# The first stage of a two-layer hybrid backbone: loads and stores put in another order on one queue

## The chip, the cores and the metric

The kernel runs on one core of one Trainium2 chip. The metric is device time in microseconds. A core has TensorE (matmul, PE in the profile), VectorE (DVE), ScalarE (ACT), GpSimd (POOL), and SyncE (SP), whose queue issues the DMAs of this kernel. The engines run their own instruction lists in order and meet through semaphores.

## The reference

The reference is a two-layer backbone over 1024 latent tokens and 256 context tokens of width 1024. Cut to what matters here:

```python
sc, scc = silu(c), silu(c_ctx)
# layer 0: convolution branch and gated linear recurrence, side by side
shift, scale, gate = split(sc @ mod_w[0] + mod_b[0], 3)
hx = rmsnorm(x, norm_g[0]) * (1 + scale) + shift
hc = rmsnorm(ctx, norm_g[0]) * (1 + scale_c) + shift_c      # same weights, from scc
z = hx @ ev_w_in                       # va, vg, ga, xb, gb
y_a = silu(layernorm(conv31(va * sigmoid(vg)))) * silu(ga)
y_b = rglru(conv4(xb), h0=from context) * silu(gb)
x = x + gate * (concat(y_a, y_b) @ ev_w_out)
# layer 1: pooling mixer
u, g = split(h @ od_w_in, 2)
d = multiscale_pool(u)                 # 4 groups
y = einsum("bngi,gij->bngj", d, od_w_grp) * od_scale
x = x + gate * ((y * silu(g)) @ od_w_out)
return rmsnorm(x, final_g)
```

Pooling is linear, so the kernel multiplies the `u` half of `od_w_in` with `od_w_grp` ahead of time; this product is called the fold. Two of its four groups are folded in the first stage.

## The kernel before, in words

Matrix products run in a split form: a 32-bit operand becomes a high and a low part (`split`, L102: ScalarE casts the high part, VectorE or GpSimd subtracts to get the low one), and a product is three matmuls: high by high, high by low, low by high.

Almost all of the text is about the first stage, L274 to L435, which ends with the first matmuls of the even layer (L672 on). What it does:

- Fold of groups 0 and 1 (`fold`, L238). A group loads two matrices `graw`, splits them into `gh` and `gl`, and then takes four weights `wu`, each of which is loaded and split by `wload` (L117) and used for two products of 12 matmuls (L260 to L262). A product is copied from PSUM by ScalarE (`fo`, L265) and stored to DRAM (`wfold`). Group 0's low parts come from VectorE, group 1's from GpSimd. `fold` is a generator; `fold_some(n)` runs its next n pieces, and a group has five: the group matrices, and one piece a weight.
- Tokens. `x_load` (L365) loads 128 of the 1024 columns of `x` as a tile `x_k`, and sums squares on ScalarE and VectorE. `rstd_cols` (L197) turns the sums into factors spread over all partitions (`ms_x`): column sums on TensorE, the root on ScalarE (`rc_x`), a diagonal on VectorE (`dg_x`), and one matmul.
- Modulation. `mod_loads` (L318) loads a block of `mod_w` and multiplies it with the SiLU of `c` and `c_ctx` (`modr`); `mod_cols` (L330) copies the result to a row (`modrow`), turns it into columns (`modt`), and writes shift and scale into `m0` and `a0`. There are four blocks of four loads, and each serves two token tiles. `modulate` (L343) writes the split tokens `h0h` and `h0l`.
- Context tokens. `ctx_load`, `ctx_scale` and `ctx_split` (L381 to L394) do the same for the 256 context tokens: `sq_c` is their root, `cx` the tokens, `cth` and `ctl` the split parts.
- The even layer's first weights: `xb`, whose product is made for latent tokens (`xb`) and context tokens (`xbc`), then `vg` and `va`. `uc` is the short convolution of `xb`; it is split into `uh` and `ul` for the gate products `g`.
- Gate dots. The third part of the first layer's modulation, which nothing reads before the output projection, is made by eight VectorE dot products of `modT` tiles with the SiLU of `c`, spread over all partitions (`cL`). Before, the spread is made at the very front by two matmuls (L378), and the dots run in the even layer's first turn (L711 to L718), where their tiles are those of the recurrence (`l`).

The order of the work is set in two ways. A scheduler orders the instructions of each engine by its own estimate of times. On SyncE's queue, loads made by `load` (L109) in the first stage are chained: each is issued after the load that stands before it in the program. The fold's stores are not part of that chain; they are put on the queue by the scheduler. From L444 on, the order on VectorE, ScalarE, GpSimd and TensorE is that of the program (`on`, L440).

Weights go through a pool of two buffers for each kind: raw (`wr`), high (`wh`) and low (`wl`). A load of a raw weight is issued once the raw weight two places ahead has been split.

Of the kernel before, what the change touches and what calls it, by code (L numbers as in the profile page):

```python
# [56 lines left out]
def body(ctx, tc, xT, ctxT, cc, ccol, modT, modW, win, gw, wout, wu, grp, wg, wo1, small, edge, ident, outT):  # L57
# [49 lines left out]
    chain = [None]  # L107

    def load(out, src):  # L109
        with ExitStack() as lctx:  # L110
            if chain[0] is not None:
                lctx.enter_context(tc.issue_after(chain[0].ins))
            d = nc.sync.dma_start(out, src)
            if chain[0] is not None:
                chain[0] = d
# [29 lines left out]
    nc.sync.dma_start(sm, small)  # L145
    eg = base.tile([P, 4 * 16], F32, name="eg")
    nc.sync.dma_start(eg, edge)
# [23 lines left out]
    nc.scalar.activation(sa, lam, AF.Abs)  # L171
    nc.scalar.activation(sa, sa, AF.Exp, scale=-1.0)
    nc.vector.tensor_scalar(out=sb, in0=sa, scalar1=2.0, scalar2=None, op0=add)
    nc.vector.reciprocal(sb, sb)
    nc.vector.tensor_tensor(out=sz, in0=sa, in1=sb, op=mult)
    nc.vector.tensor_tensor(out=sb, in0=sz, in1=sz, op=mult)
    nc.vector.memset(sa, 1.0 / 17.0)
    for n in range(7, -1, -1):
        nc.vector.tensor_tensor(out=sa, in0=sa, in1=sb, op=mult)
        nc.vector.tensor_scalar(out=sa, in0=sa, scalar1=1.0 / (2 * n + 1), scalar2=None, op0=add)  # L180
    nc.vector.tensor_tensor(out=sa, in0=sa, in1=sz, op=mult)
    nc.vector.tensor_scalar(out=sb, in0=lam, scalar1=-1.0, scalar2=0.0, op0=mult, op1=ALU.max)
    nc.vector.scalar_tensor_tensor(out=sa, in0=sa, scalar=2.0, in1=sb, op0=mult, op1=add)
    nc.vector.tensor_scalar(out=chalf, in0=sa, scalar1=4.0, scalar2=None, op0=mult)
    nc.vector.tensor_scalar(out=cneg, in0=sa, scalar1=-8.0, scalar2=None, op0=mult)
# [52 lines left out]
    def fold(g, raw_tile, out_tile, g_tile=None, w_tile=None):  # L238
        g_tile = g_tile or dtile
        gh, gl = [], []  # L240
        for i in range(2):
            raw = raw_tile(f"graw_{g}_{i}")
# [10 lines left out]
        for kp in range(KT // 2):  # L253
            wh, wl = (wload(wu[g, kp], f"wu_{g}_{kp}", nc.vector if g == 0 else nc.gpsimd)
                      if w_tile is None else ws[kp])
            for s in range(2):
                ps = psum(f"fold_{g}_{kp}_{s}")
                for i in range(4):
# [7 lines left out]
                (nc.sync if g < 2 else nc.scalar).dma_start(dst[:, :, s, :].rearrange("m p c -> p m c"),  # L266
                                    o.rearrange("p (m c) -> p m c", c=P))
# [4 lines left out]


# [5 lines left out]
    with ExitStack() as sctx:  # L279
# [117 lines left out]
        for k in range(3):  # L397
            x_load(k)
# [1370 lines left out]
```

## Time and profile before

| | us |
|---|---|
| time, median of 3 runs | 1304.87 |
| the three runs | 1301.92, 1304.87, 1305.92 |
| the profiled execution's own time | 1306.04 |
| its span, first to last instruction | 1304.0 |
| TensorE busy in the span | 1267.2 (97%) |
| VectorE busy | 1132.8 (87%) |
| ScalarE busy | 646.1 (50%) |
| GpSimd busy | 300.2 (23%) |

A row of the timeline gives start and duration in us, the engine and the line, the operation, output and inputs by the program's names, shapes, count, and in brackets the idle time before it and what ended that. In the views by windows the columns are the window, and for each engine its busy time and instructions; then the granted TensorE clock (1.00 is full speed), the busy share of the DMA engines, and GB/s. A row whose engine ends in q (SPq) is an issue on a queue, not the transfer. In the list of DMA issues the last figure of a row is the median time from issue to landing. The mean granted clock of the profiled execution is 0.993.

### The profile page before, as it was taken

The numbers are of one execution on the slowest core, as the hardware profiler recorded it, in microseconds if no ns is written. First come the engines' busy times: TensorE is split into PE (matmuls) and PEld (weight loads), VectorE is DVE, ScalarE is ACT, GpSimd is POOL, SyncE is SP. The second block draws the span as 40 slices with busy tenths as digits, with TensorE's granted clock in tenths as the row PEclk, the third lists the DMA queues.
The fourth block names the chain that finished last, engine by engine and source line by source line (L and its number), as shares of the span: only waits on it lengthen the run. The fifth ranks groups of instructions, "written<-read, shape, count | busy, mean of one in ns | idle before, by whom it ended". The sixth has DMA issues, their size and how long they took to land.

```text
span 1304.0 us, 16066 instructions
## 1 busy us (share of the span) xinstructions
PE 1267.2 (97%) x5780; PEld 1036.4 (79%) x5780; DVE 1132.8 (87%) x1756; ACT 646.1 (50%) x935; POOL 300.2 (23%) x151
## 2 busy tenths in 40 slices
PE   7999999999999999999999999999999999999995
PEld 5687888888888887888887778788888888788784
DVE  6669999999999999978968959999999987977776
ACT  7443666566566633236535346634343434645442
POOL 0212644364535546543210022000000000000002
PEclk9999999999999999999999999999999999999997
DMA  9953111122011233442418566334333334868623
GB/s 360 337 178 112 57 42 64 52 62 69 37 57 57 81 127 124 154 145 89 147 47 287 181 195 178 106 121 154 121 126 101 121 113 137 309 217 281 214 85 129
DMA packets 82865, 181.81 MB, mean 139 GB/s; under 512 B 7777, under 2 KB 27617, under 8 KB 82786
## 3 DMA queue, kind: packets, MB, share of 16 engines
q1 hardware_dynamic: 74338, 176.60, 39.9%
q10 hardware_dynamic: 8448, 4.20, 1.1%
q8 instruction: 45, 0.74, 0.2%
q14 instruction: 34, 0.28, 0.1%
HBM read 136.72 MB, written 44.04 MB: 139 GB/s over the span
## 4 chain that ended last, share of the span: by engine, by line
PE 55%; DVE 29%; DMA 8%; issue 3%; ACT 3%; POOL 1%; SPq 0%; POOLq 0%; ACTq 0%; DVEq 0%
DVE conv L444 7%; PE wob L444 6%; PE vg L444 5%; PE va L444 4%; PE xb L444 4%; DVE l L444 4%; PE g L444 3%; DMA yr_t<-y_t 2%; PE fold L262 2%; PE fold L260 2%; PE fold L261 2%; PE ga L135 2%; PE ga L444 2%; PE ga L134 2%; PE ga L136 2%
## 5 line engine op out<-in xcount | busy, mean ns | idle before, releaser
L444 DVE SCALAR_TENSOR_TENSOR conv<-u,sm,conv 128x505 f32<-128x505 f32 (+6 forms) x224 | 153.5, 745 | 1.0
L1588 POOL TENSOR_TENSOR o<-x,rr 128x256 f32<-128x256 f32 (+1 forms) x9 | 8.0, 925 | 452.6 <-ACT rr L1576 449.6
L444 ACT ACTIVATE l<-g,sm 128x512 f32<-128x512 f32 (+1 forms) x96 | 58.7, 618 | 60.0 <-PE g L444 59.2
L104 POOL TENSOR_TENSOR wl_wu<-wr_wu,wh_wu 128x1024 fp32r<-128x1024 f32 x12 | 28.7, 2390 | 171.5 <-ACT wh_wu L103 128.1
L260 PE MATMUL fold<-gh,wh_wu 128*128 128x512 f32 x128 | 53.2, 416 | 4.9 <-ACT wh_wu L103 4.9
L444 POOL TENSOR_TENSOR l<-l,l 128x1280 f32<-128x1280 f32 x16 | 47.1, 2965 | 25.6 <-ACT l L444 15.1
L444 PE MATMUL wob<-ybl,wh_wob 128*128 128x512 f32 x128 | 50.1, 392 | 2.3 <-POOL ybl L444 2.3
L261 PE MATMUL fold<-gl,wh_wu 128*128 128x512 f32 x128 | 51.7, 404 | 0.0
L262 PE MATMUL fold<-gh,wl_wu 128*128 128x512 f32 x128 | 50.3, 405 | 0.3 <-POOL wl_wu L104 0.3
L444 PE MATMUL gb<-h0h,wl_gb 128*128 128x512 f32 x128 | 49.9, 390 | 0.2 <-POOL wl_gb L444 0.2
L444 PE MATMUL gb<-h0l,wh_gb 128*128 128x512 f32 x128 | 49.8, 389 | 0.0
L444 PE MATMUL wob<-ybh,wh_wob 128*128 128x512 f32 x128 | 49.8, 389 | 0.0
L444 PE MATMUL gb<-h0h,wh_gb 128*128 128x512 f32 x128 | 49.8, 389 | 0.0
L444 PE MATMUL vg<-h0h,wh_vg 128*128 128x512 f32 x128 | 49.8, 389 | 0.0
L444 PE MATMUL vg<-h0l,wh_vg 128*128 128x512 f32 x128 | 49.8, 389 | 0.0
L444 PE MATMUL wob<-ybh,wl_wob 128*128 128x512 f32 x128 | 49.8, 389 | 0.0
L444 PE MATMUL vg<-h0h,wl_vg 128*128 128x512 f32 x128 | 49.8, 389 | 0.0
L444 PE MATMUL va<-h0h,wh_va 128*128 128x512 f32 x128 | 49.8, 389 | 0.0
L444 PE MATMUL va<-h0l,wh_va 128*128 128x512 f32 x128 | 49.8, 389 | 0.0
L444 PE MATMUL va<-h0h,wl_va 128*128 128x512 f32 x128 | 49.8, 389 | 0.0
L444 DVE TENSOR_TENSOR_SCAN l<-l,l 128x256 f32<-128x256 f32 (+1 forms) x32 | 48.7, 1521 | 1.1
L103 ACT CAST wq_g<-wr_g 128x512 fp32r<-128x512 f32 x48 | 28.2, 620 | 40.9 <-DVE wr_g L887 12.9
(593 smaller groups left out, 4291.4 us busy)
## 6 DMA issues: line engine op xcount, KB each, us to landing
wr_wu<-wu SPq DMA_DIRECT2D x16, 512.0 KB, 4.5
modw<-modW SPq DMA_DIRECT2D x16, 512.0 KB, 7.1
x_part<-xp SPq DMA_DIRECT2D x32, 256.0 KB, 2.4
mod<-modT SPq DMA_DIRECT2D x32, 256.0 KB, 3.7
wr_v<-wfold SPq DMA_DIRECT2D x16, 512.0 KB, 3.6
wr_g<-wg SPq DMA_DIRECT2D x16, 512.0 KB, 4.4
wr_wo<-wo SPq DMA_DIRECT2D x16, 512.0 KB, 4.6
yr_t<-y_t SPq DMA_DIRECT2D x16, 512.0 KB, 5.9
```

The source lines that it names most:

```text
L103: return (nc.scalar.copy(hi, src), eng.tensor_tensor(out=lo, in0=src, in1=hi.bitcast(F32), op=sub))
L104: eng.tensor_tensor(out=lo, in0=src, in1=hi.bitcast(F32), op=sub))
L134: nc.tensor.matmul(ps, hi[:, kc], xh[k][:, cols], start=(k == 0), stop=False)
L135: nc.tensor.matmul(ps, hi[:, kc], xl[k][:, cols], start=False, stop=False)
L136: nc.tensor.matmul(ps, lo[:, kc], xh[k][:, cols], start=False, stop=(k == ks - 1))
L260: nc.tensor.matmul(ps, wh[:, kc], gh[i], start=(i == 0), stop=False)
L261: nc.tensor.matmul(ps, wh[:, kc], gl[i], start=False, stop=False)
L262: nc.tensor.matmul(ps, wl[:, kc], gh[i], start=False, stop=(i == 3))
L444: last[eng] = f(*args, **kw)
L1588: nc.gpsimd.tensor_tensor(out=o[:, k - k0], in0=v, in1=rr, op=mult)
```

## The change

It changes the first stage and moves two pieces of work into it or within it:

- The front of the queue becomes: group matrix, first fold weight, second group matrix, second fold weight, two token tiles, third fold weight, and so on. The small tables (`sm`, `eg`, `idx`) go to later places, and with `sm` the decay rates of the recurrence, now a function called in the middle of the stage.
- The fold's stores of groups 0 and 1 are no longer placed by the scheduler. They are collected in a list, and `store_folds(n)` puts the next n on the chained queue: group 0's after later weights, group 1's eight all together at the end of the stage.
- A modulation block's four loads are made in one piece, after the two `modulate` calls of the block before; some of the last block's loads take buffers of another pool.
- `xb` is loaded ahead of group 1's last fold weight; `vg` and `va` are loaded within the chain of the first stage.
- The gate dots move from the even layer's first turn to the end of the first stage, and take token buffers. `cL` is loaded from DRAM as a broadcast instead of being spread by matmuls.
- Ten small matmuls on a tile of ones run at the start. The low part of group 1's first weight goes to VectorE. Two pools get more buffers (6 to 8, and 6 to 7).

Cut to its core (the decay rates are the same instructions, now within `decay_rates()`):

```diff
@@ fold @@
-        gh, gl = [], []
+        gh, gl, early = [], [], None
         for i in range(2):
+            if g == 0 and i == 1:
+                early = wload(wu[g, 0], f"wu_{g}_0", nc.vector)
             raw = raw_tile(f"graw_{g}_{i}")
             load(raw, grp[g, i])
...
-            wh, wl = (wload(wu[g, kp], f"wu_{g}_{kp}", nc.vector if g == 0 else nc.gpsimd)
-                      if w_tile is None else ws[kp])
+            if kp == 0 and early is not None:
+                wh, wl = early
+            elif w_tile is None:
+                wh, wl = wload(wu[g, kp], f"wu_{g}_{kp}", nc.vector if g == 0 or kp == 0 else nc.gpsimd)
+            else:
+                wh, wl = ws[kp]
...
-                (nc.sync if g < 2 else nc.scalar).dma_start(...)
+                if g < 2:
+                    stores.append((dst, o))
+                else:
+                    nc.scalar.dma_start(dst, o)
...
+    def store_folds(n):
+        while n and stores:
+            load(*stores.pop(0))
+            n -= 1
...
+        warm = psum("warm")
+        for i in range(10):
+            nc.tensor.matmul(warm[:, :P], ones, ones, start=True, stop=True)
+
+        def spread_c():
+            load(cL, cc[0].partition_broadcast(P))
+            nc.scalar.activation(cL, cL, AF.Silu)
+
+        def gates():
+            for m in range(2 * KT, 3 * KT):
+                raw = xtile(f"mod0_{m}")
+                load(raw, modT[0, m])
+                nc.vector.scalar_tensor_tensor(out=raw, in0=raw, scalar=1.0, in1=cL, op0=mult, op1=mult,
+                                               accum_out=m0[:, 0, m : m + 1])
...
-        fold_some(2)
-        for k in range(3):
+        fold_some(3)
+        for k in range(2):
             x_load(k)
         fold_some(1)
-        for k in range(3, 7):
+        load(ccv, ccol)
+        nc.scalar.activation(cpad[:, :, 0:2], ccv, AF.Silu)
+        for k in range(2, 5):
             x_load(k)
+        store_folds(2)
         fold_some(1)
-        x_load(7)
-        mod_loads(0, range(3))
+        load(idx, ident)
+        load(sm, small)
+        for k in range(5, 8):
+            x_load(k)
+        store_folds(2)
+        mod_loads(0, range(2))
+        fold_some(1)
+        mod_loads(0, range(2, 4))
         rx = [rstd_cols(acc[h][:, :H], f"x{h}", idx, spool, h) for h in range(2)]
         fold_some(1)
-        mod_loads(0, range(3, 4))
+        store_folds(4)
         mod_cols(0)
...
+        mod_loads(1, range(4))
+        decay_rates()
         fold_some(1)
+        mod_cols(1)
         modulate(2)
         modulate(3)
+        mod_loads(2, range(4))
         fold_some(1)
+        mod_cols(2)
         modulate(4)
         modulate(5)
+        mod_loads(3, range(4))
+        w_xb0 = wload(win[3 * KT], "xb0", nc.vector)
         fold_some(1)
+        mod_cols(3)
         modulate(6)
         modulate(7)
-        w_xb0 = wload(win[3 * KT], "xb0", nc.vector)
         ctx_load(0)
         ctx_load(1)
+        w_vg0 = wload(win[KT], "vg0", nc.vector)
         ctx_scale()
         ctx_split(0)
         ctx_split(1)
-        chain[0] = None
+        raw_va0 = wpool.tile([P, D], F32, tag="wr", name="wr_va0")
+        load(raw_va0, win[0])
+        spread_c()
+        store_folds(8)
+        gates()
+        load(eg, edge)
+        chained[0] = False
```

More of the change, by code (lines that the diff above doesn't have):

```diff
@@ L294, in fold_some @@
                 next(folds, None)
-        cx = [spool.tile([P, D], F32, name=f"cx_{i}") for i in range(2)]
+        cx = []
         xs = []
@@ L677, in body @@
         mm3(xc, w, (ch, cl), slice(0, C))
-        w = wload(win[KT], "vg0", nc.gpsimd)
+        w = w_vg0
         uc = utile("uc0")
```

80 lines of the change are left out of this document (28 added, 52 removed).

## The prediction

> **What bounds the kernel now.** I read the page's busy times and slices first, then TensorE's timeline of the first 125 us, then the other engines' timelines and the queue's at the same places, and last the windows for the clock.
>
> ```profile
> span 1304.0 us, 16066 instructions
> ...
> PE 1267.2 (97%) x5780; PEld 1036.4 (79%) x5780; DVE 1132.8 (87%) x1756; ACT 646.1 (50%) x935; POOL 300.2 (23%) x151
> ...
> PE   7999999999999999999999999999999999999995
> ```
>
> TensorE is the bound, but its busy share says little, since a matmul's record overlaps the next one's. So I go by the distance from one start to the next, and by the points of the first stage at which the changed kernel can be compared with this one.
>
> ```profile
> 10.29 0.80 PE L260 MATMUL fold<-gh,wh_wu 128*128 128x512 f32 x1 [2.90 <-ACT wh_wu L103]
> ...
> 15.15 0.63 PE L260 MATMUL fold<-gh,wh_wu 128*128 128x512 f32 x1
> 15.58 0.63 PE L261 MATMUL fold<-gl,wh_wu 128*128 128x512 f32 x1
> ...
> 17.20 0.39 PE L260 MATMUL fold<-gh,wh_wu 128*128 128x512 f32 x1
> 17.43 0.39 PE L261 MATMUL fold<-gl,wh_wu 128*128 128x512 f32 x1
> ...
> 45.85 1.07 PE L326 MATMUL modr<-modw,cpad 128*32 128x256 f32 x16
> ...
> 51.52 0.95 PE L335 MATMUL modt<-sm,modrow 128*128 128x2 f32 x8
> ...
> 53.30 0.50 PE L260 MATMUL fold<-gh,wh_wu 128*128 128x512 f32 x1 [0.27 <-ACT wh_wu L103]
> ...
> 55.77 0.50 PE L262 MATMUL fold<-gh,wl_wu 128*128 128x512 f32 x1 [0.27 <-POOL wl_wu L104]
> ...
> 72.38 0.48 PE L260 MATMUL fold<-gh,wh_wu 128*128 128x512 f32 x1
> ...
> 89.30 0.28 PE L134 MATMUL xbc<-cth,wh_xb 128*128 128x256 f32 x1
> ...
> 97.40 0.28 PE L135 MATMUL xbc<-ctl,wh_xb 128*128 128x256 f32 x1
> 97.52 0.28 PE L136 MATMUL xbc<-cth,wl_xb 128*128 128x256 f32 x1
> ...
> 103.56 0.39 PE L444 MATMUL va<-h0h,wl_va 128*128 128x512 f32 x1
> ...
> 117.69 0.39 PE L444 MATMUL xb<-h0h,wl_xb 128*128 128x512 f32 x1
> 119.97 0.50 PE L444 MATMUL g<-uh,wh_gw 128*128 128x512 f32 x1 [1.89 <-DVE u L444]
> ```
>
> The reader is to see three things. A 512-column matmul starts 0.227 us after the one before (17.20 to 17.43), but 0.43 us after it at first (15.15 to 15.58): the thirteen steps from 10.29 on lose 2.9 us. From 10.29 on TensorE hardly waits: 0.27 us twice in those rows, and 2.28 - 0.23 = 2.05 us ahead of 119.97. A step of 256 columns is 0.12 us (97.40 to 97.52). And after the first stage TensorE stands at nine tenths or more in every slice but the last, so what the first stage gains or loses by the `g` matmul at 119.97 is taken as the change of the time. That point is my yardstick.
>
> **The front of the queue.** The loads go on one queue in program order.
>
> ```profile
> 0.74 0.40 SPq L145 DMA_DIRECT2D sm<-small  x1
> ...
> 3.85 0.43 SPq L113 DMA_DIRECT2D wr_wu<-wu  x1
> ```
>
> ```profile
> 10.00:20.00 10.00, 9.71 (x31) 7.71 (x32) 8.35 (x15) 8.24 (x15) 0.00 (x0) 1.00 1.03 412
> ```
>
> The first fold weight is issued at 3.85 us, behind five small loads and both group matrices. In the changed kernel it is the second issue, one place of 0.47 us behind 0.74, thus 2.64 us earlier, and one 512 KB transfer less lies ahead of it: 1.27 us at 412 GB/s. The fold starts at 10.29 - 3.9 = 6.4 us, say 6.5. The vector work of the decay rates and the spread of `c` leave the front too; they delay nothing that counts, as ScalarE's cast releases the fold, not they.
>
> **The first group's fold.** Four weights of 24 matmuls, 96 x 0.227 = 21.8 us, with 0.3 us for the first low part: it ends at 28.6 us. Before, token sums and modulation matmuls lay between these; now they come behind them, as the changed order of TensorE's instructions shows.
>
> **The middle, 28.6 to 37.0 us.** Here the changed order is serial. Sums of squares, their root on ScalarE, the diagonal on VectorE, its product, the second half of the first modulation block, `modrow`, and only then the cast of the second group's first weight.
>
> ```profile
> 31.19 1.28 ACT L204 ACT_TABLE_LOAD   x1
> 32.51 0.26 ACT L204 ACTIVATE rc_x<-ms_x,eps_r 128x4 f32<-128x4 f32 x1
> ```
>
> ```profile
> 33.02 0.69 DVE L207 TENSOR_TENSOR dg_x<-idx,rc_x 128x512 f32<-128x512 f32 x1
> ```
>
> ```profile
> 50.05 0.57 ACT L332 COPY modrow<-modr 128x512 f32<-128x512 f32 x1
> ...
> 52.20 1.05 ACT L103 CAST wh_wu<-wr_wu 128x1024 fp32r<-128x1024 f32 x1
> ```
>
> Copy of the last fold 0.6, table 1.3, two roots and two diagonals of about 0.26 + 0.2 + 0.69 each, 2.3; the last diagonal's product 0.9 (an estimate: four 0.23 us passes); two loads' modulation matmuls 1.1; `modrow` 0.6; cast 1.05; some 0.1 us at each of five handovers: 8.4 us, so the second group starts at 37.0. In before the same links are hidden behind the fourth fold weight; that cover is gone. The data are there by then. A load of 512 KB that has little beside it lands 3.5 us after its issue:
>
> ```profile
> wr_xb<-win SPq DMA_DIRECT2D x4, 512.0 KB, 3.5
> ```
>
> So the first load lands at 0.74 + 3.5 = 4.2 us, and the weight, with 22.6 such blocks between (a store counts half), at 4.2 + 22.6 x 1.27 = 32.9 us, 3 us ahead of its cast.
>
> **The second group.** In the changed order a whole modulation block (16 matmuls, 2 x 1.0 us by the 45.85 row) ends ahead of each later weight, and on ScalarE `modrow` stands ahead of that weight's cast. So TensorE waits 0.57 + 1.05 + 0.1 = 1.75 us at each of three weights, where before it waited 0.27. Then it has four matmuls (0.9) and `modt` (0.95) to cover GpSimd's low part:
>
> ```profile
> 53.33 2.39 POOL L104 TENSOR_TENSOR wl_wu<-wr_wu,wh_wu 128x1024 fp32r<-128x1024 f32 x1 [7.15 <-ACT wh_wu L103]
> ```
>
> That leaves 0.6 us open at two of them; at the third weight half a modulation block fills it. First weight 37.0 + 5.44 + 0.95 = 43.4; block 2.1, wait 1.75, weight 5.44 + 0.95 + 0.6: 54.2; block, wait, weight with half a block: 65.5; half a block, wait, last weight: 75.3. Before, the last weight's 24 matmuls start at 72.38 and end at 77.8. So of 3.8 us gained at the front, and 2.9 if the slow steps go, 2.5 are left. The queue's own holds cost nothing here: the last fold weight must wait until GpSimd has split the one two places ahead (about 60.5), lands some 3.5 us later, and its cast comes at 67.3.
>
> **The context and gate dots.** `xb` takes 48 x 0.227 + 0.4 = 11.3 us and ends at 86.6 (before 89.30). What comes next needs the context tokens, and their chain doesn't come earlier:
>
> ```profile
> 81.82 0.48 ACT L193 ACTIVATE sq_c<-ms_c,eps_r 128x256 f32<-128x256 f32 x1 [1.86 <-PE ms_c L191]
> ...
> 97.84 0.57 ACT L444 ACTIVATE uc<-xbc,sm 128x256 f32<-128x256 f32 x1 [7.69 <-PE xbc L136]
> 98.31 1.20 ACT L444 ACTIVATE uc<-xb,sm 128x1024 f32<-128x1024 f32 x1
> 99.40 1.04 ACT L444 CAST wh_va<-wr_va 128x1024 fp32r<-128x1024 f32 x1
> ```
>
> ```profile
> 82.32 1.75 DVE L194 RECIPROCAL ssqc<-sq_c 128x256 f32<-128x256 f32 x1 [2.06 <-ACT sq_c L193]
> 84.11 2.36 DVE L390 TENSOR_TENSOR cx<-cx,ssqc 128x1024 f32<-128x1024 f32 x2
> ...
> 106.58 1.22 DVE L444 SCALAR_TENSOR_TENSOR l<-l,cL 128x1024 f32<-128x1024 f32 x1
> ```
>
> On ScalarE, between the last `h0h` (75.7, 0.4 after the last weight's end) and `sq_c`, the change puts a table load, `cL`'s SiLU, two fold copies, the `vg` cast and a second table load: 1.3 + 1.15 + 1.1 + 1.05 + 1.3 = 5.9, so `sq_c` ends at 82.0, as before. On VectorE reciprocal and scaling follow (85.9), then one gate dot (1.2), four context steps (1.3) and ScalarE's cast (1.05): the first `xbc` matmul can go at 89.4, where TensorE has waited 2.8 us. Five more dots stand ahead of the second `ctl`, and the changed order puts 39 instead of 24 `vg` matmuls ahead of the rest of `xbc`: 89.4 + 39 x 0.227 + 11 x 0.12, then four more `vg` (0.9) and 12 x 0.12, ends it at 102.0, against 97.6. `uc` twice and the `va` cast on ScalarE: 104.7; GpSimd's low part 2.4: 107.1, where the third `va` matmul starts; before it started at 103.56. That is 3.55 us late. In return VectorE is free when `va` is done (the dots are over at about 100), and the 2.05 us ahead of 119.97 vanish: 107.1 + 46 x 0.227 + 24 x 0.12 + 1.04 = 121.5, that is 1.5 us late.
>
> **The slow steps.** This sum has none, while the 119.97 of before has two stretches:
>
> ```profile
> 33.00:33.50 0.50, 0.50 (x5) 0.50 (x5) 0.48 (x1) 0.00 (x0) 0.00 (x0) 0.67 0.97 390
> ...
> 36.50:37.00 0.50, 0.50 (x3) 0.41 (x4) 0.00 (x0) 0.50 (x2) 0.00 (x0) 0.92 1.02 403
> ```
>
> The granted clock falls to half at about 33.2 and returns at about 36.6, 3.4 us later, after three microseconds of small matmuls. The ten new warm-up matmuls run from 1.0 to about 5.3 us, and then TensorE idles until 6.5. Bounds: they suffice, loss 0; or not, up to two stretches of 3.4 us at half speed, 3.4 us. I take 1.7, as the 10.29 row lost 2.9 after a similar burst and pause. The middle, 8.4 us with some 5 us of small matmuls in it, is more like the place where the clock fell than anything in before: 0 to 5 us (a half-speed stretch over products and first folds), and I take 0.9, half a chance of 1.7. Together 2.6. The Trainium skill ("TensorE: Matmul & The Clock Gate", Part 1) speaks against the change at this place: a free-running window of 3.4 us sets the clock, and idle windows throttle it again. The trace agrees with 33.2 to 36.6; by that rule a burst of 4.3 us holds a whole window only one time in four, which would leave the sum as it is.
>
> **Sum.** 1306.04 + 1.5 + 2.6 = 1310.1 us, in the terms of the profiled execution, which lies 1.2 us above the median of 1304.87 (runs from 1301.92). I give 1310.
>
> **Rivals.** *Clock held:* no slow stretch, 1306.04 + 1.5 = 1307.5, no change that a measurement could tell (0.3% is 3.9 us). *Clock lost often:* 3.4 at the start, 5 in the middle: 1306.04 + 9.9 = 1316; for it speak the new idle times at six places, against it that most are under 3 us. *Faster:* the front's lead survives. If ScalarE's casts and the context chain don't hold TensorE at the weights, the 3.9 us of the front, 2.9 of slow steps and the 2.05 us wait all go: 1306.04 - 8.8 = 1297.2. It decides where the waits behind `modrow` and `cth` stay under about 1 us each; against it speaks the written order of ScalarE. *The queue isn't ahead:* data land later than used, as in a stall of the last weight behind its buffer; the last fold weight's 3 us of slack must go first, so this gives a microsecond or two on top of the forecast.
>
> **Numbers.** Forecast with its neighbours 1308.8 to 1313: 0.44. Clock lost often or a late queue: 0.16. Clock held: 0.28, within 0.3%. Faster: 0.12. So faster 0.12, same 0.28, slower 0.60. The range runs from 1302, into the faster case, to 1317.
>
> **What would show it.** Right: fold from 6.5 us; waits of 1.5 to 2 us on `wh_wu` at three weights and on `cth` near 87 to 89; `va` waiting for ScalarE and GpSimd near 105; no wait for `u` before the first `g`. Wrong: fold weights of the second group without waits, `xbc` ended ahead of 97.6, or the `g` yardstick before 117 us.

## The result and the profile after

| | before | after |
|---|---|---|
| time, median of six runs each, us | 1304.35 (1301.92 to 1305.92) | 1315.53 (1313.74 to 1316.40) |
| ratio, 95% interval | | 1.0088 (1.0075 to 1.0101) |
| the profiled execution's own time | 1306.04 | 1315.56 |
| yardstick: start of the `g` matmul | 119.97 | 128.76 |

The change makes the kernel 11.2 us slower. Forecast were 1310 us, 4.1 over the profiled execution of before, and a range from 1302 to 1317: the direction and the range held, the size was less than half. Between the two profiled executions the time grows by 9.5 us, and 8.8 of them are there at the yardstick. The page of after says as little as that of before: the same busy time of TensorE in a span 9.5 us longer.

```profile
span 1313.5 us, 16075 instructions
...
PE 1267.3 (96%) x5796; PEld 1039.3 (79%) x5796; DVE 1128.8 (86%) x1758; ACT 648.6 (49%) x937; POOL 293.0 (22%) x149
...
PE   9889999999999999999999999999999999999995
```

TensorE's timeline of after, at the points that the prediction named (start, duration, engine, line, operation; in brackets the idle time before it and what ended it):

```profile
6.76 0.50 PE L266 MATMUL fold<-gh,wh_wu 128*128 128x512 f32 x1 [1.57 <-ACT wh_wu L103]
7.10 0.39 PE L267 MATMUL fold<-gl,wh_wu 128*128 128x512 f32 x1
...
28.78 0.39 PE L268 MATMUL fold<-gh,wl_wu 128*128 128x512 f32 x1
...
37.55 0.50 PE L266 MATMUL fold<-gh,wh_wu 128*128 128x512 f32 x1 [1.70 <-ACT wh_wu L103]
...
47.80 0.50 PE L266 MATMUL fold<-gh,wh_wu 128*128 128x512 f32 x1 [1.70 <-ACT wh_wu L103]
...
58.60 0.50 PE L266 MATMUL fold<-gh,wh_wu 128*128 128x512 f32 x1 [1.65 <-ACT wh_wu L103]
...
68.99 0.50 PE L266 MATMUL fold<-gh,wh_wu 128*128 128x512 f32 x1 [1.65 <-ACT wh_wu L103]
...
76.99 0.50 PE L134 MATMUL xb<-h0h,wh_xb 128*128 128x512 f32 x1 [0.69 <-DVE x L362]
...
91.94 0.39 PE L134 MATMUL xbc<-cth,wh_xb 128*128 128x256 f32 x1 [3.31 <-ACT cth L103]
...
102.69 0.28 PE L135 MATMUL xbc<-ctl,wh_xb 128*128 128x256 f32 x1
...
106.24 0.28 PE L136 MATMUL xbc<-cth,wl_xb 128*128 128x256 f32 x1
...
109.26 0.50 PE L482 MATMUL va<-h0h,wh_va 128*128 128x512 f32 x1 [1.57 <-ACT wh_va L482]
...
111.69 0.79 PE L482 MATMUL va<-h0h,wl_va 128*128 128x512 f32 x1 [1.71 <-POOL wl_va L482]
112.29 0.63 PE L482 MATMUL va<-h0h,wh_va 128*128 128x512 f32 x1
...
128.76 0.40 PE L482 MATMUL g<-uh,wh_gw 128*128 128x512 f32 x1
```

Up to 69 us the rows stand within a microsecond of the forecast: first fold, first group's end, second group, and the three waits behind `modrow`. From `xb` on they drift. The waits for `cth` and for `va`'s two parts are where they were expected, but `xbc` ends at 106.4 instead of 102.0, and behind the waits the steps are longer (112.29 comes 0.60 after 111.69). The windows name the reason. Their columns are the stretch, its length, busy time of PE, PEld, DVE, ACT and POOL, the granted clock, the DMA share and GB/s:

```profile
93.00:97.00 4.00, 4.00 (x13) 3.11 (x12) 4.00 (x7) 1.04 (x1) 0.00 (x0) 0.57 0.92 357
110.00:118.00 8.00, 6.30 (x16) 4.96 (x17) 4.01 (x3) 4.31 (x6) 4.24 (x3) 0.57 0.11 33
```

By windows of one microsecond the clock is at half from 93.3 to 96.7 and from 110.3 to 117.2. The first stretch begins 1.4 us behind the wait for `cth`, the second within the second wait for `va`. By the steps they cost 1.6 us (nine from 93.09 to 96.73, at 0.227 each otherwise) and 2.4 us (fourteen from 111.69 to 117.30); for the rest of the second stretch TensorE idles. Nothing of the kind is there in the middle of this execution, where before had its stretch at 33 to 37.

What holds `cth` and `ctl` is read on ScalarE and VectorE:

```profile
78.14 1.28 ACT L393 ACT_TABLE_LOAD   x1
79.44 1.06 ACT L393 ACTIVATE cL<-cL 128x1024 f32<-128x1024 f32 x1
...
82.42 1.28 ACT L193 ACT_TABLE_LOAD   x1
83.72 0.47 ACT L193 ACTIVATE sq_c<-ms_c,eps_r 128x256 f32<-128x256 f32 x1
90.84 1.04 ACT L103 CAST cth<-cx 128x1024 fp32r<-128x1024 f32 x1 [6.65 <-DVE cx L373]
```

```profile
88.29 1.22 DVE L399 SCALAR_TENSOR_TENSOR mod<-mod,cL 128x1024 f32<-128x1024 f32 x1
...
95.46 1.22 DVE L104 TENSOR_TENSOR ctl<-cx,cth 128x1024 fp32r<-128x1024 f32 x1
96.60 1.22 DVE L399 SCALAR_TENSOR_TENSOR mod<-mod,cL 128x1024 f32<-128x1024 f32 x1
...
98.89 1.22 DVE L104 TENSOR_TENSOR ctl<-cx,cth 128x1024 fp32r<-128x1024 f32 x1
```

The gate dots (`mod<-mod,cL`) stand between the context's own steps; six of the eight come ahead of the second `ctl`. TensorE doesn't wait for that: `ctl` is done at 100.1, and TensorE takes it at 102.69, behind 39 `vg` matmuls that its own order puts there.

### The profile page after: what moved, and what is told of

It is laid out like the page before. It is cut to its first block, busy times and chain, and to the rows that moved or that the text cites. A ratio compares the mean times of both kernels' runs of the same rounds, so it can differ in the third digit from the quotient of the medians.

```text
span 1313.5 us, 16075 instructions
## 1 busy us (share of the span) xinstructions
PE 1267.3 (96%) x5796; PEld 1039.3 (79%) x5796; DVE 1128.8 (86%) x1758; ACT 648.6 (49%) x937; POOL 293.0 (22%) x149
## 4 chain that ended last, share of the span: by engine, by line
PE 45%; DVE 31%; DMA 13%; issue 4%; ACT 4%; POOL 2%; SPq 1%; POOLq 0%; DVEq 0%; ACTq 0%
DVE conv L482 6%; PE wob L482 6%; PE va L482 5%; PE vg L482 5%; PE xb L482 4%; DVE l L482 3%; PE g L482 3%; DMA wr_wu<-wu 2%; DVE ws L1336 2%; DMA yr_t<-y_t 2%; PE ga L482 2%; PE ga L134 2%; PE ga L135 2%; PE ga L136 2%; DMA wr_v<-wfold 1%
```

## The experiments

Theory End: the gate dots, and ScalarE's work on `cL`, hold the context's chain at the stage's end; TensorE waits, and the waits cost clock. Theory Columns: the loss is the three waits of 1.7 us in the second fold group. Theory Queue: it is the order of transfers. The experiments were timed in five sessions on five chips, each kernel beside the kernel before on the same chip (medians of before from 1304.65 to 1305.76 us); the row of after is the measurement of the result. "Over before" is the difference of the medians, so rows that differ by a microsecond or two can't be told apart; the yardstick is that of one profiled execution, whose own time stands beside it. The two differ by 1184 to 1190 us in every kernel but two, so the yardstick carries the time to some 3 us either way.

| kernel | ratio to before (95%) | over before, us | yardstick | own time |
|---|---|---|---|---|
| after | 1.0088 (1.0075 to 1.0101) | 11.2 | 128.76 | 1315.56 |
| dots_back | 1.0031 (1.0015 to 1.0047) | 4.6 | 121.80 | 1309.83 |
| dots_behind_ctl | 1.0031 (1.0020 to 1.0042) | 3.5 | 128.63 | 1319.01 |
| before_dots_moved | 1.0055 (1.0041 to 1.0069) | 6.5 | 125.69 | 1314.62 |
| xbc_after_vg | 1.0021 (1.0008 to 1.0034) | 3.1 | 122.96 | 1309.26 |
| back_xbc_late | 1.0031 (1.0015 to 1.0046) | 3.8 | 120.92 | 1307.10 |
| keep_busy | 1.0045 (1.0028 to 1.0063) | 6.6 | 124.39 | 1313.82 |
| c_early | 1.0089 (1.0058 to 1.0119) | 11.4 | 139.59 | 1326.85 |
| cast_first | 1.0064 (1.0046 to 1.0081) | 9.1 | 126.31 | 1312.62 |
| blocks_split | 1.0153 (1.0135 to 1.0172) | 18.7 | 136.49 | 1320.57 |
| stores_free | 1.0233 (1.0213 to 1.0253) | 32.1 | 147.19 | 1331.75 |
| no_warm | 1.0088 (1.0073 to 1.0104) | 11.6 | 129.14 | 1312.70 |
| front_only | 1.0053 (1.0038 to 1.0068) | 7.3 | 124.82 | 1312.53 |
| front_early | 1.0043 (1.0029 to 1.0058) | 6.4 | 122.31 | 1309.35 |
| before_warm | 1.0013 (1.0000 to 1.0027) | 2.0 | 119.61 | 1309.26 |
| combined | 1.0013 (0.9998 to 1.0028) | 2.5 | 121.15 | 1309.19 |
| combined_keep | 1.0041 (1.0025 to 1.0056) | 6.3 | 122.37 | 1307.61 |
| before_dots_after_u | 1.0247 (1.0218 to 1.0277) | 32.4 | 115.47 | 1340.72 |
| after_dots_after_u | 1.0290 (1.0259 to 1.0320) | 38.5 | 118.07 | 1343.64 |

### The gate dots

dots_back takes `gates()` out of the stage and puts the eight loads and dots back into the first turn.

```diff
-        gates()
...
+            if state is None:
+                for m in range(2 * KT, 3 * KT):
+                    part = L[m % 6][:, :D]
+                    nc.sync.dma_start(part, modT[0, m])
```

> The changed kernel (1315.5 us, median) with one part undone: the eight gate dots and their loads go back into the even layer's first turn; all the rest stays. Theory End: the loss lies at the end of the first stage, where five dots stand on VectorE ahead of the second ctl and the sixteen us of dots delay uc and with it va; without them the first xbc still waits for cth (ScalarE's table loads and SiLU of c stay, only the first dot's 1.2 us goes: 3.3 us becomes about 2.1), but xbc ends near 101 instead of 106.4, va's low part no longer comes last, and half of the half-clock time goes; the dots come back as 2 us of waiting for u. Expected 1308 to 1311. Theory Columns: the loss is the waits of 1.65 us at three weights of the second fold group, behind modrow; they stay, so the time stays at 1315 within 1 us. Theory Queue: the loss is the order of the transfers (stores and loads on one queue); taking eight loads out of the queue's end, behind everything that is awaited, changes nothing: 1315 within 1 us.

dots_behind_ctl leaves them in the stage and forbids one thing, that VectorE takes a dot ahead of the context's second `ctl`:

```diff
+                    gctx.enter_context(tc.issue_after(ctl_done[1].ins))
                     nc.vector.scalar_tensor_tensor(out=raw, in0=raw, scalar=1.0, in1=cL, op0=mult, op1=mult,
```

> The changed kernel (1315.5 us) with only VectorE's order changed: the eight gate dots stay in the first stage with their loads, but none goes ahead of the context's second ctl. If the dots cost by holding the context (Theory End in its first part): the first dot's 1.2 us leaves the wait for cth (3.3 becomes 2.1) and five leave the way to ctl, xbc ends 3 to 6 us earlier and the half clock behind the wait may go: 1309 to 1312. If they cost by holding uc and the u products behind: 1314 to 1317, as the same ten us then stand there.

before_dots_moved is the converse: the kernel before, with the dots and their loads written behind `ctx_split(1)`.

> The kernel before (1304.4 us) with one part done alone: the eight gate dots and their loads move from the even layer's first turn to the end of the first stage, behind the context's split. Theory End: the dots now stand ahead of the second ctl or of uc on VectorE; xbc's last steps come 3 to 6 us later, va with them, the 2.05 us of waiting for u go, and a wait of over 2 us opens which may halve the clock: 1306 to 1311. Theories Columns and Queue: the dots cost nothing there and free VectorE ahead of u: 1302 to 1304.5.

All three say End. Of 11.2 us, 4.6 are left without the dots in the stage and 3.5 with them behind `ctl`; so some 7 us hang on their place between the context's steps, and not on where their loads or the `u` products stand.

How they cost is less simple than waiting for VectorE. Where `xbc`'s matmuls stand among `vg`'s is set by the scheduler, by its own estimate of times, so an edit on VectorE's dots changes TensorE's order too. Between `xbc`'s first matmul and its second stand 39 `vg` matmuls in after (and four more ahead of its last eleven), but 18 in dots_back and in dots_behind_ctl:

```profile
92.33 0.38 PE L134 MATMUL xbc<-cth,wh_xb 128*128 128x256 f32 x1 [2.17 <-ACT cth L103]
...
96.68 0.28 PE L135 MATMUL xbc<-ctl,wh_xb 128*128 128x256 f32 x1
```

These rows are dots_back's. In after five `vg` matmuls are left to cover the way from `xbc`'s end over `uc` and the cast of `va`, and TensorE waits 1.57 and 1.71 us; in dots_back and dots_behind_ctl 30 are left, and `va` isn't waited for. The dots are what starts this, but the two ways, VectorE's delay and the order made from it, are not separated by these three runs.

Moved alone into the kernel before, the dots cost 6.5. There VectorE takes all eight ahead of the context's reciprocal (89.00 us), so they hold the chain at an earlier step, and TensorE's timeline shows the largest wait; behind its beginning the clock falls too:

```profile
95.56 0.58 PE L134 MATMUL xbc<-cth,wh_xb 128*128 128x256 f32 x1 [7.45 <-ACT cth L103]
```

```profile
91.00:99.00 8.00, 3.44 (x9) 2.79 (x10) 7.06 (x12) 2.09 (x2) 0.00 (x0) 0.57 0.00 0
```

### TensorE's order, and its idle time

xbc_after_vg makes the context's matmuls come behind the first half of `vg` (24 matmuls that need nothing from the context); the dots stay.

```diff
-        mm3(xc, w, (ch, cl), slice(0, C))
...
             all_of(mm3_fixed(vg[0], w, (hh, hl), HALF[0]))
+            if j == 0:
+                xc = psum("xbc0")[:, :C]
+                all_of(mm3_fixed(xc, wx, (ch, cl), slice(0, C)))
```

> The changed kernel (1315.5 us) with one edit in TensorE's order: the context's 24 xbc matmuls come behind vg's first half instead of ahead of it. Nothing else is moved, and the gate dots stay. Theory End, with the order as the cause: TensorE does vg's 24 matmuls (5.4 us) while cth is made, so the 3.3 us of waiting go and with them the half clock near 93 to 97; xbc then ends near 97 to 99 unless the second ctl, behind five dots, comes at 97 and holds it; va still waits for ScalarE and GpSimd by 1 to 2 us: 1308 to 1312. If the chain of the context behind the dots binds whatever TensorE does first: 1313 to 1315.5.

keep_busy puts matmuls that nobody reads into the wait; the text of the kernel moves nothing else.

```diff
+        keep = psum("keep")
+        for i in range(14):
+            on("pe", nc.tensor.matmul, keep, w_xb0[0][:, :P], hh[0][:, :H], start=True, stop=True)
```

> The changed kernel (1315.5 us) with fourteen 128x512 matmuls into an unused bank put between xb's last matmul and xbc's first, 3.2 us of work in a wait of 3.3 us; nothing waits for them. Theory End with the clock as part of it: TensorE is no longer idle from 88.5 to 91.9, so the stretch of half clock near 93 to 97 goes; xbc ends 1.7 us earlier, and the time is 1313 to 1314. If the clock's fall has nothing to do with the wait: the same stretch, 1315.5. Theories Columns and Queue: 1315.5, and up to 0.3 more if the filling overruns the wait.

back_xbc_late joins dots_back and xbc_after_vg.

> The changed kernel (1315.5 us) with both repairs: dots and their loads back in the first turn (alone 1309.4), xbc's matmuls behind vg's first half (alone 1308.6). If they take away the same stretch (TensorE's wait for the context and the clock lost after it): 1307 to 1309. If they add: 1302 to 1304.

xbc_after_vg gives back 8 us with one edit, near the good end of what was expected. VectorE's order is that of after, dots included; so TensorE's order alone can take the loss away. Its timeline shows the dots again, now at `ctl`, but TensorE waits 4.26 us in all, against 3.31 + 1.57 + 1.71 = 6.59 in after, `va` isn't waited for, and the windows from 93 to 118 us are at full clock:

```profile
97.84 0.39 PE L482 MATMUL xbc<-ctl,wh_xb 128*128 128x256 f32 x1 [2.53 <-DVE ctl L104]
...
101.27 0.39 PE L482 MATMUL xbc<-ctl,wh_xb 128*128 128x256 f32 x1 [1.73 <-DVE ctl L104]
```

In keep_busy the wait's length is the same, only filled, and 4.6 us come back. Both stretches are at full clock, the second one too, behind a wait for `va` that shrank to 0.43 us:

```profile
93.00:97.00 4.00, 3.86 (x18) 2.87 (x17) 4.00 (x10) 1.81 (x2) 0.00 (x0) 1.00 1.02 415
110.00:118.00 8.00, 8.00 (x36) 6.60 (x37) 3.00 (x3) 3.21 (x4) 3.64 (x2) 1.00 0.21 52
```

It doesn't separate the clock from all else, though, for TensorE's order changed here too: 29 `vg` matmuls stand ahead of `xbc`'s last eleven, not 43. From `xb`'s start to the yardstick the profiled execution takes 44.4 us against 51.8: of these 7.3 us, 14 x 0.227 = 3.2 are the order, 1.6 and 2.6 the two stretches. (Its `xb` starts 2.9 us later than after's, behind two stretches at half clock, from 7 to 11 and from 51.5 to 55.5 us.)

That a long wait costs clock rests on more traces. In the first 180 us of the profiled executions, once the fold has begun, TensorE has eleven waits of 2.97 us or more, and at each the clock is at half in the wait or just behind it: 2.97 in no_warm, 3.31 in after, 3.37 in front_only, 4.83 and 4.96 in blocks_split, 5.00 and 6.43 in stores_free, 7.45 in before_dots_moved, 7.55 in cast_first, 10.55 and 10.54 in before_dots_after_u and after_dots_after_u. Shorter waits go both ways: no stretch behind the 2.17 us in dots_back or the 2.53 in xbc_after_vg, but one behind the 1.93 us at `u` in back_xbc_late (122 to 126 us, behind its yardstick).

back_xbc_late stays where each part alone is: they remove the same stretch and don't add.

### The other theories

cast_first puts `modrow`'s copy behind the next fold weight's cast on ScalarE.

```diff
+                if b:
+                    mctx.enter_context(tc.issue_after(casts[-1].ins))
                 nc.scalar.copy(row, modr[b])
```

> The changed kernel (1315.5 us) with ScalarE's order at three places: the copy of modrow comes behind the next fold weight's cast instead of ahead of it; loads and blocks stay as they are. Theory Columns: the three waits of 1.65 us at 47.8, 58.6 and 69.0 go (the cast then hides behind the block's last matmuls), 4 to 5 us in all, and all of it reaches the end: 1310.5 to 1311.5. Theory End: xb ends 3 to 5 us earlier, but cth hangs on the last h0h, ms_c, ScalarE's table loads and VectorE; these come earlier by what the last modt comes earlier, 2 to 4 us, the wait at cth grows by the rest: 1312 to 1314.

blocks_split divides the column blocks around the weights (`mod_loads(1, range(2))`, `fold_some(1)`, `mod_loads(1, range(2, 4))`, and one and three loads for block 2).

> The changed kernel (1315.5 us) with the modulation's column blocks 1 and 2 divided around the fold weights again, as before (two loads ahead of one weight and two behind it; one and three). Theory Columns: the waits of 1.7 us on the fold weight's cast at 47.8 and 58.6 us go, 3.3 us, and all of it reaches the end: 1312 or less. Theory End: the second group ends 3 us earlier, but sq_c follows ScalarE's work and the context's chain, which hangs on the last h0h; whatever TensorE gains is waited for at cth, 88 us, as far as the context's chain does not come earlier too: 1313 to 1315.5. Theory Queue: no change, 1315.

stores_free issues the sixteen stores where the scheduler puts them (`nc.sync.dma_start(dst, o)` in place of `stores.append((dst, o))`).

> The changed kernel (1315.5 us) with the sixteen stores of the folded groups 0 and 1 taken out of the written order: each is issued where the scheduler puts it, as before. Theory Queue: the stores a weight later or at the end are what costs; 1308 to 1312. Theory End: TensorE's waits on cth, va and the casts are not made by transfers, and the clock's stretches stay: 1313 to 1317.

Columns isn't the main cause: dots_back and xbc_after_vg keep all three waits (1.65 to 1.70 us in their traces) and take back 7 to 8 us. What the waits cost by themselves isn't shown. Cutting two of the three in cast_first (0.47 and under 0.3 us; the third stays at 1.56) gave 2 us in the median, and the intervals of cast_first and after overlap. In its trace the last weight starts 3.1 us earlier than in after (65.85 against 68.99), a stretch at half clock from 67 to 74.5 us takes 1.9 of it back, and VectorE now takes five gate dots instead of one ahead of the context's first modulation, so that `cth` comes 2.9 us later than in after and TensorE waits for it:

```profile
94.87 0.58 PE L136 MATMUL xbc<-cth,wh_xb 128*128 128x256 f32 x1 [7.55 <-ACT cth L103]
```

blocks_split was meant for the same question and doesn't answer it. With half of a block behind the weight, `modt` and the two `modulate` steps come after the weight's matmuls instead of under them, and on ScalarE the next weight's cast stands behind their `h0h`, so that TensorE gets two longer waits (ScalarE's timeline, then TensorE's):

```profile
58.41 1.15 ACT L365 ACTIVATE h0h<-x,m 128x1024 fp32r<-128x1024 f32 x1 [0.17 <-DVE x L362]
59.46 1.03 ACT L103 CAST wh_wu<-wr_wu 128x1024 fp32r<-128x1024 f32 x1
```

```profile
60.55 0.80 PE L266 MATMUL fold<-gh,wh_wu 128*128 128x512 f32 x1 [4.83 <-ACT wh_wu L103]
...
79.45 0.80 PE L266 MATMUL fold<-gh,wh_wu 128*128 128x512 f32 x1 [4.96 <-ACT wh_wu L103]
```

Queue falls, as far as the stores go, with the opposite sign: in the changed kernel their written order pays. Without it the same kernel loses another 21 us; a store that waits for ScalarE's copy holds the queue from 36 to 45 us, the modulation loads behind it come late, and TensorE waits for data (queue, then TensorE):

```profile
35.09 1.03 SPq L113 DMA_DIRECT2D modw<-modW  x2
45.28 0.38 SPq L274 DMA_DIRECT2D wfold<-fo  x1
45.70 2.17 SPq L113 DMA_DIRECT2D modw<-modW  x2
```

```profile
51.06 1.08 PE L341 MATMUL modr<-modw,cpad 128*32 128x256 f32 x8 [5.00 <-DMA modw<-modW]
```

c_early loads the row of `c` behind `ccv`, spreads it with two matmuls and takes its SiLU at the front.

> The changed kernel (1315.5 us) with only the way of c put back: its row is loaded behind ccv, spread by two matmuls and passed through SiLU at the front, so that no table load, SiLU and second table load (1.28 + 1.06 + 1.28 us) stand between the last h0h and sq_c on ScalarE. The gate dots stay at the stage's end. Theory End: sq_c comes 2 to 3 us earlier (then at the end of ms_c's matmul, not behind ScalarE's queue), cth with it, and the wait of 3.3 us ahead of xbc falls below 1.5; the dots still delay the second ctl, uc and va: 1310 to 1313. If the dots alone made the loss: 1314.5 to 1315.5. Theory Columns: 1315.5.

It stays open. Its six runs lie between 1312.0 and 1326.9 us; in the profiled one the clock fell at half a dozen places in the fold, TensorE came so late that `cth` was waiting for it, and nothing can be said on ScalarE's share. The order is that of after, with 39 and four `vg` matmuls, and `va` is waited for by 1.57 and 1.71 us without any wait at `cth`.

### The front

no_warm has one warm-up matmul in place of ten. front_only is the kernel before with the early first weight, the late small loads and the warm-up; front_early has the fourth weight's load earlier and `decay_rates()` behind `modulate(1)`. before_warm is the kernel before with ten warm-up matmuls.

> The changed kernel (1315.5 us) with one instead of ten matmuls on the constant ahead of the first fold weight. If they are what keeps the first fold at 0.23 us a step, the fold starts at the same 6.7 us but its first thirteen or so steps take 0.43 us, and the first group ends 2 to 3 us later; whether that reaches the end depends on the chain through the middle, which follows the first group's last fold: 1317 to 1318.5. If the slow steps before had another cause: 1315.5.

> The kernel before (1304.4 us) with only the front of the queue and the warm-up done: the first fold weight second in the queue, the second one behind two token loads, the small loads, the spread of c and the decay rates behind it, ten matmuls ahead. Blocks, stores, the fourth fold weight as cover of the middle, and the gate dots stay as before. Theory End: the front's 3.5 us and the slow steps' 2.9 us are real and were lost behind; with nothing else changed they reach the end as far as VectorE's dots ahead of u let them: the yardstick comes at 114 to 118 us and the time is 1298 to 1302.5. If what follows (the context's chain, the dots) holds TensorE at the same times whatever the front does: 1303.5 to 1305.

> As front_only (1313.1 us), the kernel before with the front of the queue and the warm-up alone, but the fourth fold weight behind one modulation load and not three, and the decay rates on VectorE 30 us later, so that the weights' buffers come free. If the fourth weight's lateness and the clock lost behind it made front_only slow: the wait of 3.4 us at 23.8 goes, and 1299 to 1304 is left. If the front's lead is lost whatever the loads do, at the first token sums, the context and the dots: 1304 to 1308.

> The kernel before (1304.4 to 1305.8 us) with the ten warm-up matmuls alone. The fold starts at 10.3 us, some 5 us after the warm-up's end. If the first steps at 0.43 us come from TensorE having been idle or new to the clock: with the pause of 5 us they stay slow, or go in part; 2.9 us at most. If what is gained there reaches the end: 1302 to 1305; if the front is not on the path (as the changed kernel without its warm-up says, where the median hardly moved): 1304 to 1306.

```profile
6.74 0.79 PE L266 MATMUL fold<-gh,wh_wu 128*128 128x512 f32 x1 [4.89 <-ACT wh_wu L103]
7.33 0.63 PE L267 MATMUL fold<-gl,wh_wu 128*128 128x512 f32 x1
...
95.67 0.38 PE L134 MATMUL xbc<-cth,wh_xb 128*128 128x256 f32 x1 [2.97 <-ACT cth L103]
```

These rows are no_warm's: without the burst the first steps are 0.43 us again. With it they are 0.23 in after, but not always: in keep_busy and c_early, whose front is the same, the clock is at half from about 7 to 11 us. The 11.6 us over before, against 11.2, can't be told apart. That doesn't show that the front is off the path. In no_warm's trace the second group starts at 39.23 us against 37.55, and the first `xbc` matmul at 95.67 against 91.94 (two stretches at half clock, at 51.5 and 75 us, add to it); the yardstick comes near after's only because the stretch behind `va` isn't there, 14.5 us from the third `va` matmul against 17.1. In before_warm the fold starts at 11.96, 1.7 us later than in before, and its first steps take 0.43 us all the same.

front_early starts the fold at 6.8 us, 3.5 ahead of before, and is at the yardstick 2.3 us behind it; in its trace the clock is at half from 15.2 to 18.6 and from 32.2 to 35.7, the wait for `cth` is 1.41 us and that for `u` 1.89. No part of the front alone made the kernel before faster; all expectations of a gain there were wrong.

### In search of a faster kernel

combined has dots_back, c_early, xbc_after_vg and cast_first in one; combined_keep adds four 128x128 matmuls ahead of the second group. before_dots_after_u and after_dots_after_u have the dots behind the two `u` products, through scratch tiles 4 and 5 (`L[4 + m % 2]`).

> The changed kernel (1315.5 us) with what the runs so far point to: the gate dots and their loads back in the first turn, c spread by matmuls at the front, the xbc matmuls behind vg's first half, and the fold weights' casts ahead of modrow. The first group starts at 6.8 us and its fold has no slow steps. Theory End: no wait of over 2 us is left behind the middle (28 to 37 us), the second group ends 4 us earlier, so the yardstick, 119.97 before and 128.8 after, comes at 112 to 116 us: 1296 to 1302, faster than both kernels, if VectorE's dots ahead of u (which now come against an earlier va) don't take back 2 to 4 us; with that, 1301 to 1304. If the loss is in the order of the transfers: 1309 or above, as with the dots alone put back.

> The combined kernel (1308.0 us: dots back in the first turn, c spread at the front, xbc behind vg's first half, casts ahead of modrow) with four 128x128 matmuls on the constant between the first modulation block and the second group's first weight, 1.65 us of work in a wait of 1.7 us; nothing waits for them. If the half clock seen there near 35 to 48 us comes from TensorE standing idle in the middle: part of the 5 us lost goes, 1303 to 1306. If the small matmuls of the modulation themselves let the clock fall: 1308, unchanged.

> The kernel before (1304.4 to 1305.8 us) with the eight gate dots behind the first turn's two u products instead of ahead of them, through two of the six scratch tiles. If the 2.05 us that TensorE waits for u ahead of 119.97 are on the path: they go, 1302.5 to 1304. If something else is as late, or the dots hold the next turn's uc on VectorE: 1304.5 to 1308.

> The changed kernel with the dots behind the first turn's u products, and xbc behind vg's first half. TensorE has no wait of over 2 us left behind the middle but the three of 1.7 us at the fold weights. If the waits at cth, va and u make the loss: 1304 to 1307, 1 to 3 us under back_xbc_late. If VectorE then holds the next turn: 1307 to 1310.

None beats the kernel before. combined comes nearest, with an interval that holds no change; its profiled execution lost the clock from 35.3 to 38.7 and from 42.2 to 49.0. The filling in combined_keep didn't help: its median is 3.7 us higher. The two last ones show how a good yardstick can mislead. In before_dots_after_u the wait for `u` is gone and `g` starts at 115.47, 4.5 us earlier than before; but with two tiles the dots wait for their loads one by one and take VectorE from 112.4 to 133.4 us, the convolution's steps stand ahead of `uc` in the written order, ScalarE waits for `uc`, and the cast of the next weight, for which TensorE waits 10.55 us, stands behind that:

```profile
162.00 1.26 ACT L444 CAST uh<-uc 128x1280 fp32r<-128x1280 f32 x1 [23.50 <-DVE uc L444]
...
163.65 1.03 ACT L444 CAST wh_xb<-wr_xb 128x1024 fp32r<-128x1024 f32 x1
```

## Why the prediction was right in direction and short in size

**The front.** Forecast 6.5 us, found 6.76; the 1.7 us for slow steps there were not lost, and the first group ended at 29.0 (forecast 28.6). That the fold began at full speed is one execution's: in keep_busy and c_early the clock fell at this place, so the half chance taken wasn't idle. Whether the lead counts at the end stays open: no_warm's median doesn't show the loss, its trace does up to `va`.

**Middle and second group.** 37.0 forecast, 37.55 found; three waits of 1.75 forecast, 1.70, 1.65 and 1.65 found; the 0.9 us of slow clock taken there were not in this trace, but kernels with the same middle have such a stretch in theirs (39.5 to 43.5 us in dots_back, 32 to 36 in xbc_after_vg). The sizes were right.

**`xb` and the context.** `xb` starts 1.7 us later than forecast, 0.69 of it a wait for VectorE that the text left out: `xb` needs the bank from which the last `modulate` still reads `ms_x`. `sq_c` ends at 84.2 against 82.0, the first `xbc` matmul starts at 91.94 against 89.4. The 2.5 us enter ahead of `sq_c`: the last `h0h` ends at 78.1, not at 75.7, since VectorE adds four of the context's square sums (69.59 to 73.2 us) between the last `modt`, done at 71.0, and the last `modulate`, and the sum had left these out. From there on the chain took the time forecast. The 39 `vg` matmuls in TensorE's order, and what follows from them at `va`, were in the prediction.

**The clock.** With its 2.6 us of slow steps the forecast had the yardstick at 124.1; it came 4.7 us later. 2.5 are the context chain's, and most of the rest is the clock's, the term that failed in its mechanism: 2.6 us were put at the start and in the middle, none behind the waits at `cth` and `va` that the same text forecast. In the profiled execution it measured 0 there and 1.6 and 2.4 us here, 4.0 in all. 121.5 + 2.5 of context chain + 1.8 by which `xbc` took longer than its 12.6 + 0.2 at `va` + 2.7 by which the stretch from 111.69 to 128.76 exceeds its forecast of 14.4 is 128.7; the trace has 128.76. So the step that failed is the one that priced the waits at `cth` and `va` by their length alone, beside the square sums left out of the context's chain. The eleven waits of 2.97 us and more, each with its stretch at half clock, show that a wait of this length carries a clock cost; keep_busy, where the wait is filled, has no such stretch. That `va`'s two shorter waits bring theirs by the same cause is likely, not shown: in no_warm waits of 0.84 and 1.71 us at this place had none.

**The end.** `va` waited for ScalarE and GpSimd, and the wait for `u` vanished, as said. Behind the yardstick another 0.7 us was lost, within what the kernels of the table scatter.

**Profile and median.** The sum went from the profiled execution of before, 1306.04, which lay 1.7 us above its median of six runs; that of after lies on its median. So 1.7 of the 11.2 us is no term of the sum.

**Rivals.** The rival of a clock lost often gave 1316 us, near the 1315.5 measured, but with the stretches at the wrong places: as a sum it is right by luck. Against it the text had said that most idle times are under 3 us; that was no protection, as the last section shows.

**What stays open.** With the dots out of the way, or `xbc` set late, 3 to 5 us over before are left. The three waits behind `modrow`, a stretch at half clock that comes at one place or another, and the front may each have a share; no run gives it. combined, which has all the repairs, is at 2.5, with an interval that holds no change.

## What to carry to other kernels

Work that nobody awaits still has a price where an engine that runs its list in order takes it between the steps of a chain that TensorE awaits, and where the scheduler then rearranges TensorE's own list: put it behind the chain's last step (one ordering edge gave back some 7 us here, TensorE's order changing with it), or give TensorE work that doesn't need the chain. After such an edit, read the order of the other engines too, for it may have moved. A forecast wait of about 3 us on TensorE must carry its clock with it: count the wait, and then up to half of the 3.4 to 7 us behind it. A lead at the front of a stage may be lost further on, as front_early's 3.5 us were; and a load or a store that stands on the queue ahead of an awaited one, and waits itself, can cost more than the lead.

## What the runs showed of the hardware

The clock fell behind waits of 1.7 us as well. In the profiled execution of dots_behind_ctl, the slowest of its eight runs (the others lie between 1305.9 and 1310.7), it did so after each of the second group's weights:

```profile
37.53 0.50 PE L266 MATMUL fold<-gh,wh_wu 128*128 128x512 f32 x1 [1.71 <-ACT wh_wu L103]
...
50.95 0.50 PE L266 MATMUL fold<-gh,wh_wu 128*128 128x512 f32 x1 [1.70 <-ACT wh_wu L103]
...
78.06 0.50 PE L266 MATMUL fold<-gh,wh_wu 128*128 128x512 f32 x1 [1.65 <-ACT wh_wu L103]
```

```profile
38.00:46.00 8.00, 8.00 (x27) 6.57 (x26) 6.36 (x11) 2.89 (x3) 0.00 (x0) 0.57 1.02 408
52.00:60.00 8.00, 7.86 (x26) 6.40 (x25) 5.63 (x10) 2.88 (x3) 1.35 (x1) 0.57 0.20 78
```

The group's period is 13.5 us here, 10.3 to 10.8 in after with the same waits and the same order. So one order of instructions has two speeds, by some 3 us a turn, and in this execution a clock once lost was lost again at the same place of each next turn (in dots_back and keep_busy a stretch of 3.4 to 4 us in this group was not followed by another). That the longer period keeps the wait at the same phase of the clock's own window is a reading of these rows, not tested. The Trainium skill ("TensorE: Matmul & The Clock Gate", HAM oscillation — how this bites in real kernels) describes such a repeated loss for idle gaps over about 3.4 us, and a cost of half the throttled time. The cost agrees (about 7 us at half clock and a turn 2.7 to 3.2 us longer here); the gap doesn't: the clock fell behind 1.65 to 1.71 us, with 1 to 1.9 us of small modulation matmuls ahead of them.

A gate dot of 1.22 us took 3.40 us in the same execution, where GpSimd's `wl_va` (2.74 us) began 0.4 us ahead of it. The Trainium skill ("SBUF — State Buffer", Who interferes with whom) says that a VectorE instruction with two inputs in SBUF and a GpSimd instruction that reads SBUF exclude each other; the rows agree: the dot ends 1.07 us behind `wl_va`.

```profile
109.19 1.22 DVE L403 SCALAR_TENSOR_TENSOR mod<-mod,cL 128x1024 f32<-128x1024 f32 x1
...
110.34 3.40 DVE L403 SCALAR_TENSOR_TENSOR mod<-mod,cL 128x1024 f32<-128x1024 f32 x1
```

```profile
109.93 2.74 POOL L486 TENSOR_TENSOR wl_va<-wr_va,wh_va 128x1024 fp32r<-128x1024 f32 x1 [29.46 <-ACT wh_va L486]
```
